# A second seven-product group in the output projection, and a new order of each layer's last stretch

## The chip, the cores and the metric

The program runs on one core of a Trainium2 chip. The metric is the device time of one execution in microseconds, as the median of the runs shown; less is better. TensorE is called PE below, VectorE DVE, ScalarE ACT, GpSimd POOL and SyncE SP, as in the profile.

## The reference, cut to what matters

Two layers of a decoder trunk over 256 tokens and 2048 features, all in float32. Each layer ends with three branch products, a merge with sigmoid gates, and one output projection:

```python
y_a = (dsa_attention(...) * jax.nn.silu(za)) @ w_a_out
y_b = (conformer_conv(...) * jax.nn.silu(zb)) @ w_b_out
y_c = (stick_breaking_attention(...) * jax.nn.silu(zc)) @ w_c_out
g = jax.nn.sigmoid(gates).reshape(b, s, N_BRANCH, D_MODEL)
merged = g[:, :, 0] * y_a + g[:, :, 1] * y_b + g[:, :, 2] * y_c
return x + merged @ w_out                    # (256, 2048) @ (2048, 2048)
```

After the second layer comes a final RMSNorm. The change is in how `merged @ w_out` is computed, and in what stands around it.

## The kernel before, in words

**Precision.** A float32 product is made of three float32r products: each weight block is split on the chip into a high part `wh` (ACT, a cast, line 255 in `high`) and a low part `wl` (DVE, a subtraction, line 259 in `low`), each activation into `hi` and `lo`, and PE adds hi x wh, lo x wh and hi x wl (`mult`, line 270).

**Steps.** The work on weights is a list of steps which `run` goes through in order. A step takes one 512 KB weight block (2 x 128 rows, 512 columns). A plain step (`plain`) is a full one: two halves of the tokens, so 3 x 2 x 2 = 12 matmuls of 128x128x512, the last 4 of which read `wl`. `run` asks for the loads some 7 steps ahead (into 5 `raw` buffers and, each sixth, `va`) and splits the blocks 2 steps ahead. `wh` and `wl` have 3 buffers each, so the split of a step can be written only when PE has read that of the step three before.

**Seven products.** `Seven` computes a 2 x 2 x 2 block product (1024 rows, two halves of the tokens, two chunks of 512 columns) by seven products M1 to M7 in place of eight. Each is cut into two half steps, a and b, of 6 matmuls each, the last 2 of which read `wl`. A half step needs a split of its own, and the group needs sums of weight blocks (`first_sums`, `second_sum`, `last_sum`: by DVE, or by a DMA that accumulates, issued by POOL, depending on `adds` and `room`) and sums of activations (`osums`, from `output_sums`). Its four PSUM banks are X, Y, Z and W: ACT copies X to Y after M1 and W to an SBUF tile after M5, and DVE makes Z after M6 and W after M7 (`fork`, line 581), each from that tile and Y.

**The output projection before.** It has four chunks of 512 columns, q = 0 to 3. One group `o` takes the upper 1024 rows of two chunks (`p0` and `p0 + 1`: 2 and 3 in the first layer, 0 and 1 in the last); their lower rows are plain steps. The other two chunks, `c` and `d`, are 8 plain steps each, in PSUM tiles of two banks (`wide_accs`). In the last layer the lower half of chunk 3 is done after `run`, in a tail that ends with the norm and the stores.

**What comes just ahead.** The products with `w_b_out` (`y1`, 4 chunks of 4 plain steps; the last is called y15 below) and the gates' group `h1` with its plain steps `e1` and `f1`. When a chunk of `y1` is done, `merged` multiplies and adds on DVE (lines 1568, 1569), transposes on DVE (line 299, two rows), goes through DRAM by POOL's DMAs (`z`, then `zy`), and is split by ACT and DVE (`use_m`, line 668) into `mx`, which the output projection reads.

**The order.** The order of the steps is written out by hand in strings for `gather`. From there a scheduler sets the order on each engine; an engine goes through its own instructions strictly in that order. SP and POOL issue the DMAs from queues of the same kind.

Of the kernel before, what the change touches and what calls it, by code (L numbers as in the profile page):

```python
# [30 lines left out]
LATER = 10  # L31
# [20 lines left out]
def trunk(ctx: ExitStack, tc: tile.TileContext, x, w_in, xt, w_a, w_b, w_c, w_out,  # L52
# [73 lines left out]
    def part(b, i, k, n=1, ts=slice(0, S)):  # L126
        return b[k // 4][:, k % 4:k % 4 + n, i, ts]
# [178 lines left out]
    def back(z, y):  # L306

        nc.gpsimd.dma_start(y.rearrange("p (t a) k i -> p t (a k i)", a=4), z.rearrange("t b c a e -> (b c) t (a e)"))  # L308

    def turned(srcs, use, later=LATER, tmp=None, soon=False):  # L310


        n = len(srcs)
        if tmp is None:
            tmp = tp.tile([P, n * 512], F32, tag="zt", bufs=1, name=nm("zt"))
        c = srcs[0].shape[1]
        z = away([v.rearrange("p (k e) -> p k e", e=P) for v in srcs], tmp[:, :n * c], soon)
# [110 lines left out]
    def plain(w, k0, c0, act, banks, start, stop, nk=2):  # L428
        st = Step(lambda: raw_unit(w, k0, c0), None)

        def mm(w_):
            for i, j in ((0, 0), (1, 0), (0, 1)):
                for t, bank in enumerate(banks()):
                    for k in range(2):
                        a = part(act, i, k0 + k, 1, slice(t * P, (t + 1) * P))[:, 0, :]
                        m = mult(bank, a, w_[j][:, k, :], start and i + j + k == 0, stop and j == 1 and k == 1)
            return m

        st.mm = mm
# [19 lines left out]
    class Seven:  # L459


        def __init__(self, w, cols, act, sums, lead=7, own=None, adds=False, room=None):
            self.banks = banks = {}
            self.steps = {}

            def bank(n):
                if n not in banks:
                    banks[n] = acc_tile()
                return banks[n]

            self.bank = bank
# [117 lines left out]
    def gather(spec, **named):  # L589

        lists = {n: list(v) for n, v in named.items() if isinstance(v, list)}
        out = []
        for word in spec.split():
            n, _, many = word.partition("*")
            if n in lists:
                for _ in range(int(many or 1)):
                    out.append(lists[n].pop(0))
            else:
                g, p = n.split(".")
                out += [named[g][p, h] for h in range(2)] if len(p) == 2 else [named[g][p[:2], "ab".index(p[2])]]  # L600
        assert not any(lists.values()), {n: len(v) for n, v in lists.items()}
        return out
# [166 lines left out]
    for layer in range(DEPTH):  # L769
        w = w_in[layer]  # L770
# [4 lines left out]
        sums = parts(KC)  # L775
# [429 lines left out]
        def turn_first():  # L1205
            with in_turn():
# [6 lines left out]
                   g=u, y=keys, c=ug, d=ua))  # L1213
# [162 lines left out]
        room = [once(lambda: slot().rearrange("p a b -> p (a b)")) for _ in range(2)]  # L1376
# [12 lines left out]
        qs = chunk_steps(w, O_QC + 4 * P, hx, KD, lambda a: turned(a, partial(use_q, 4)))  # L1389
# [85 lines left out]
        def sticks(stick=stick, attended=attended):  # L1475
            while len(attended) < 2 * NT:
                yield 1
            for h0 in range(0, NH, 4):
# [5 lines left out]
                   g=kg, q=qs, y=za, c=kc_, d=kd_, z=zb, v=vs))  # L1484
# [86 lines left out]
        for j in range(2):  # L1571
            g = chunk_N(w, [(O_G + j * 512, 512)], hx, KD)
# [6 lines left out]
        last = layer == DEPTH - 1  # L1579
# [44 lines left out]
        wc, wb, wo = w_c[layer], w_b[layer], w_out[layer]  # L1624
# [9 lines left out]
        def merged(b, j, y):  # L1634
            sg = held.pop((b, j), None)
            with in_turn() if b == 1 else nullcontext():
                merge(b, j, y, sg)
            if b == 1:
                with in_turn():
                    turned([mg(j, t) for t in range(NT)], partial(use_m, j), LATER - 3 * (j == 3 and not last), soon=True)  # L1640

        kept_x, acc3 = {}, once(wide_accs)

        def output(q, banks, k0):
            if last and q == 3:
                return [plain(wo, k, q * 512, mx, acc3, k == 0, False) for k in range(0, KC, 2)]

            def finished():
                xc = kept_x.pop(q)
                emit_x(xc, banks(), q, q * 512, list(range(NT)))  # L1650
                store_x(xc, q * 512)

            def ask():
                kept_x[q] = residual(q * 512, 512)

            banks = once(banks or wide_accs)
            steps = [plain(wo, k, q * 512, mx, banks, k == 0, k == KD - 2) for k in range(k0, KD, 2)]
            steps[-1].at(1, finished).at(-4, ask)
            return steps

# [25 lines left out]
        p0 = 0 if last else 2  # L1686
        osums = Lazy(2, lambda: parts(4)[0])
# [9 lines left out]
        h1, e1, f1 = gates(1, 2, 7, None, 2)  # L1697
        y0, y2, y1 = ([products(b, wy, j, gx) for j in range(4)] for b, wy, gx in ((0, w_a[layer], ga), (2, wc, gc), (1, wb, gb)))
# [14 lines left out]
        zg["M4", 1].at(1, partial(gate_summed, 0))  # L1713
        zg["M3", 1].at(1, partial(gate_summed, 1))
        for i in range(2):
            y1[3][i].at(0, partial(output_sums, i * 2, i * 2 + 1))
        if last:
            zd[3].at(0, lambda: nc.sync.dma_start(fwl[0], fnw.partition_broadcast(P)))
        o = Seven(wo, (p0 * 512, p0 * 512 + 512), mx, osums, 10, None, 3)
        qs = {}  # L1720
        for q in range(4):
            own = q in (p0, p0 + 1)
            banks = (lambda v: lambda: [o.bank(n) for n in v])("ZW" if q - p0 else "XY") if own else None
            qs[q] = output(q, banks, KC if own else 0)
# [12 lines left out]
        steps += gather("y g.M1a y g.M5a g.M1b y g.M5b y g.M6a y g.M6b y g.M2a c g.M2b c g.M7a c g.M7b c g.M4a d g.M4b d g.M3a d g.M3b d",  # L1737
                        g=zg, y=y2[4:10], c=zc, d=zd)
        steps += gather(thin + rest, y=y2[10:], g=g1, c=c1, d=d1)
        steps += gather("y*2 " + begin.replace("M6a y", "M6a").replace("M2a y", "M2a") + rest, g=h1, y=y1[:8], c=e1, d=f1)  # L1740
        steps += y1[8:]
        def no_products():
            with in_turn():
                for f in halves:
# [5 lines left out]
        steps[12].at(0, lambda: urgent.__setitem__(0, True), True)  # L1750
        steps[steady - 1].at(0, lambda: urgent.__setitem__(0, False))
        steps[at_norm].at(0, norm)
        c, d = 2 - p0, 3 - p0
        if last:
            steps += qs[c][:4] + gather(
                "g.M1a d g.M5a g.M1b d g.M5b d g.M6a d g.M6b c g.M2a c g.M2b g.M7a g.M7b g.M3a e g.M3b e g.M4a f g.M4b f c*2 e*2 f*2",
                g=o, c=qs[c][4:], d=qs[d], e=qs[p0], f=qs[p0 + 1])
        else:
            steps += qs[c][:4] + qs[d][:4] + gather(
                "g.M1a c g.M5a g.M1b c g.M5b d g.M6a d g.M6b c g.M2a c g.M2b d g.M7a d g.M7b g.M3a g.M3b e g.M4a e g.M4b e*2 f*4",  # L1760
                g=o, c=qs[c][4:], d=qs[d][4:], e=qs[p0], f=qs[p0 + 1])
# [13 lines left out]
        with tc.high_priority(offset=URGENT):  # L1775
            nc.vector.reduce_sum(known, ssq[:, :, :3], axis=AX.X)
            nc.vector.tensor_scalar(half, known, -0.5 / D, -0.5 * EPS, op0=ALU.mult, op1=ALU.add)
            nc.vector.tensor_scalar(known, known, 1.0 / D, EPS, op0=ALU.mult, op1=ALU.add)

        c0, n = 1536, 512  # L1780
        xc = residual(c0, n)

        head = acc3()
        accs = [head[0], acc_tile()]
        nc.vector.tensor_add(xc[:, 1, :], head[1], xc[:, 1, :])
        oh, ol = ([slot(F32R).rearrange("p (k a) t -> p k (a t)", a=2) for _ in range(2)] for _ in range(2))
# [3 lines left out]
        for t in range(NT):  # L1790
            m, r, b = (small(1) for _ in range(3))
# [93 lines left out]
```

## Time and profile before

| | |
|---|---|
| median of 3 runs | 1980.36 us (1979.25 to 1982.67) |
| the profiled execution | 1980.07 us, its span 1978.3 us |
| PE busy in the span | 1965.0 us (99%) |
| DVE busy | 1714.5 us (87%) |
| granted PE clock over the span | 0.998 |

The time of the profiled execution is 1.8 us longer than its span, and it is 0.3 us below the median. PE's records are modelled at their ends, so how long a matmul takes is read from the distance between the starts of two groups, and where PE stood still from its waits.

### The profile page before, as it was taken

What the parts mean: (1) busy time and instruction counts of PE and PEld (TensorE: products, weight loads), DVE (VectorE), ACT (ScalarE), POOL (GpSimd) and SP (SyncE); (2) the same over time, 40 slices, a digit from 0 to 9 for tenths busy, and PEclk for the clock granted to TensorE, in tenths of its full rate; (3) what the DMA queues carried; (4) which work ended last, traced back from release to release, by engine and by line L of the source; (5) the groups of instructions that cost most, each with busy time, mean ns of one, the idle gap of its engine ahead of it and who ended that gap; (6) DMA issues with size and microseconds to landing.
All of it is one profiled execution on the core that took longest, in us unless ns stands there. A gap on an engine that the chain in (4) does not pass through costs nothing.

```text
span 1978.3 us, 26294 instructions
## 1 busy us (share of the span) xinstructions
PE 1965.0 (99%) x9170; PEld 1645.4 (83%) x9170; DVE 1714.5 (87%) x2010; ACT 1356.9 (69%) x1778; POOL 249.3 (13%) x348
## 2 busy tenths in 40 slices
PE   9999999999999999999999999999999999999998
PEld 8888887888888888888888888888888888888886
DVE  8798998988999989878786988999889988898786
ACT  7567657679888666565565666576798886665654
POOL 0021112210200002111200211122101000011010
PEclk9999999999999999999999999999999999999999
DMA  7888759876889899887978887598659798899883
GB/s 277 279 259 265 238 180 305 269 233 189 249 241 271 245 262 286 271 269 270 320 234 272 246 276 234 181 309 277 223 175 285 241 297 239 253 293 271 275 290 135
DMA packets 256261, 503.67 MB, mean 255 GB/s; under 512 B 18496, under 2 KB 31296, under 8 KB 256000
## 3 DMA queue, kind: packets, MB, share of 16 engines
q1 hardware_dynamic: 218560, 408.13, 62.2%
q0 software_dynamic: 35904, 90.72, 18.3%
q10 hardware_dynamic: 1664, 3.15, 0.4%
q8 instruction: 71, 1.16, 0.2%
q14 instruction: 62, 0.51, 0.1%
HBM read 469.16 MB, written 32.77 MB: 254 GB/s over the span
## 4 chain that ended last, share of the span: by engine, by line
PE 97%; DMA 1%; DVE 1%; ACT 0%; issue 0%; DVEq 0%; ACTq 0%
PE acc L270 66%; PE mm L270 28%; DMA raw<-in_w_in_dram 1%; PE mm L1269 1%; PE mm L1360 0%; DVE wl L259 0%; PE mm L1411 0%; PE mm L1464 0%; DMA va<-in_w_in_dram 0%; PE mm L1441 0%; PE mm L1327 0%; PE mm L918 0%; PE mm L1240 0%; PE mm L1330 0%; PE mm L1414 0%; PE mm L1469 0%
## 5 line engine op out<-in xcount | busy, mean ns | idle before, releaser
L270 PE MATMUL acc<-wh,s 128*128 128x512 f32 x3952 | 1006.1, 390 | 0.6 <-ACT wh L255 0.6
L255 ACT CAST wh<-raw 128x1024 fp32r<-128x1024 f32 (+1 forms) x637 | 665.1, 1047 | 394.0 <-PE acc L270 251.6
L259 DVE TENSOR_TENSOR wl<-raw,wh 128x1024 fp32r<-128x1024 f32 (+1 forms) x638 | 770.5, 1214 | 165.0 <-ACT wh L255 162.8
L270 PEld LDWEIGHTS acc<-wh,s 128*128 128x128 f32 x3952 | 735.2, 188 | 149.4 <-ACT wh L255 1.4
L270 PE MATMUL acc<-wl,s 128*128 128x512 f32 x1784 | 499.5, 390 | 2.3 <-DVE wl L259 2.3
L270 PEld LDWEIGHTS acc<-wl,s 128*128 128x128 f32 x1784 | 333.6, 188 | 74.1 <-DVE wl L259 5.4
L270 PE MATMUL mm<-wh,s 128*128 128x512 f32 (+1 forms) x1504 | 366.8, 385 | 0.4 <-ACT wh L255 0.4
L270 PEld LDWEIGHTS mm<-wh,s 128*128 128x128 f32 x1504 | 281.2, 188 | 55.8 <-ACT wh L255 0.9
L302 POOL DMA_DIRECT2D z<-zt x192 | 115.9, 657 | 670.8 <-DVE zt L299 626.0
L270 PE MATMUL mm<-wl,s 128*128 128x512 f32 (+1 forms) x752 | 198.0, 385 | 0.0
L270 PEld LDWEIGHTS mm<-wl,s 128*128 128x128 f32 x752 | 140.8, 188 | 26.9
L255 ACT CAST wh<-ar 128x1024 fp32r<-128x1024 f32 x92 | 97.0, 1054 | 68.3 <-PE acc L270 35.0
L259 DVE TENSOR_TENSOR wl<-ar,wh 128x1024 fp32r<-128x1024 f32 x92 | 112.1, 1222 | 23.7 <-ACT wh L255 20.6
L259 DVE TENSOR_TENSOR wl<-va,wh 128x1024 fp32r<-128x1024 f32 x53 | 64.8, 1222 | 21.8 <-ACT wh L255 21.5
L255 ACT CAST wh<-va 128x1024 fp32r<-128x1024 f32 x53 | 55.6, 1049 | 35.6 <-PE acc L270 17.2
L308 POOL DMA_DIRECT2D zy<-z x50 | 37.1, 743 | 322.2 <-DVE s L668 94.4
L270 PEld LDWEIGHTS mm<-s,wl 128*128 128x128 f32 x512 | 66.9, 191 | 5.0
L733 DVE SCALAR_TENSOR_TENSOR s<-yT,cst,s 128x256 f32<-128x256 f32 x160 | 69.8, 483 | 0.0
L270 PE MATMUL mm<-s,wl 128*128 128x192 f32 x512 | 66.0, 271 | 0.0
L728 ACT ACTIVATE ar<-yT,cst 128x256 f32<-128x256 f32 x136 | 60.5, 503 | 2.9 <-PE mm L1330 2.3
L728 ACT ACTIVATE zt<-yT,cst 128x256 f32<-128x256 f32 x128 | 57.6, 503 | 4.9 <-DVE s L1037 4.9
L530 POOL DMA_DIRECT2D ar<-in_w_in_dram x28 | 33.7, 1212 | 190.9 <-DVE wl L259 190.9
(293 smaller groups left out, 1587.0 us busy)
## 6 DMA issues: line engine op xcount, KB each, us to landing
raw<-in_w_in_dram SPq DMA_DIRECT2D x496, 512.0 KB, 4.6
raw<-in_w_out_dram SPq DMA_DIRECT2D x50, 512.0 KB, 5.4
zy<-z POOLq DMA_DIRECT2D x48, 512.0 KB, 5.9
z<-zt POOLq DMA_DIRECT2D x184, 128.0 KB, 5.3
ar<-in_w_in_dram SPq DMA_DIRECT2D x28, 512.0 KB, 6.9
ar<-in_w_in_dram POOLq DMA_DIRECT2D x28, 512.0 KB, 8.6
raw<-in_w_a_dram SPq DMA_DIRECT2D x26, 512.0 KB, 6.7
raw<-in_w_b_dram SPq DMA_DIRECT2D x26, 512.0 KB, 4.9
```

What stands on the lines that cost most here:

```text
L255: newest_parts[0] = nc.scalar.copy(u[1], u[0])
L259: newest_parts[1] = sub = nc.vector.tensor_sub(u[2], u[0], u[1].bitcast(F32))
L270: newest[0] = nc.tensor.matmul(o, lhsT, rhs, start=start, stop=stop, skip_group_check=True)
L302: nc.gpsimd.dma_start(z[:, :, :, a, :].rearrange("t b c e -> c (t b) e"), tmp[a * 32:(a + 1) * 32].rearrange("c t b k i -> c (t b) (k i)"))
L308: nc.gpsimd.dma_start(y.rearrange("p (t a) k i -> p t (a k i)", a=4), z.rearrange("t b c a e -> (b c) t (a e)"))
L530: nc.gpsimd.dma_start((homes if own is None else third)[h], block(1, 0, h), accum_op=ALU.add)
L728: nc.scalar.activation(v, yT[:, c, q:q + S], AF.Identity if bias else AF.Copy, scale=wq, **b)
L733: nc.vector.scalar_tensor_tensor(o, yT[:, c, q:q + S], wq, o, op0=ALU.mult, op1=ALU.add)
L1269: nc.tensor.matmul(ps[:, q * S:(q + 1) * S], qi[i][:, hd, :], ki[j][:, 0, :], start=n == 0, stop=n == 2)
```

## The change

A second group, `n`, does the upper 1024 rows of chunks `c` and `d`, so that all four chunks have their upper rows by seven products. `n` uses the buffers that `o` used (`ar`, `ph`, `pl`) and four single PSUM banks; `o` moves to two slots of the activations' pool (`places`, called s8 below), its first sum is partly done by an accumulating DMA (`adds` 2 in place of 3), and its banks are the halves of two wide tiles. `n` begins before `y1` is done: the last four steps of `y1` stand between its half steps. The merge of chunk 1 is asked to come back earlier, and `output_sums` moves to the steps `f1[2]` and `f1[3]`. The last layer's tail reads its bank from `n`.

```diff
-        def __init__(self, w, cols, act, sums, lead=7, own=None, adds=False, room=None):
+        def __init__(self, w, cols, act, sums, lead=7, own=None, adds=False, room=None, wide=False):
...
                 if n not in banks:
-                    banks[n] = acc_tile()
+                    if wide:
+                        banks.update(zip("XY" if n in "XY" else "ZW", wide_accs()))
+                    else:
+                        banks[n] = acc_tile()
                 return banks[n]
...
-                    turned([mg(j, t) for t in range(NT)], partial(use_m, j), LATER - 3 * (j == 3 and not last), soon=True)
+                    turned([mg(j, t) for t in range(NT)], partial(use_m, j), LATER - 3 * (j in (1, 3)), soon=True)
...
-        def output(q, banks, k0):
+        def output(q, banks):
             if last and q == 3:
-                return [plain(wo, k, q * 512, mx, acc3, k == 0, False) for k in range(0, KC, 2)]
+                return []
...
-            steps = [plain(wo, k, q * 512, mx, banks, k == 0, k == KD - 2) for k in range(k0, KD, 2)]
+            steps = [plain(wo, k, q * 512, mx, banks, False, k == KD - 2) for k in range(KC, KD, 2)]
...
-            y1[3][i].at(0, partial(output_sums, i * 2, i * 2 + 1))
+            f1[2 + i].at(0, partial(output_sums, i * 2, i * 2 + 1))
...
-        o = Seven(wo, (p0 * 512, p0 * 512 + 512), mx, osums, 10, None, 3)
+        c, d = 2 - p0, 3 - p0
+        places = [once(lambda: slot().rearrange("p a b -> p (a b)")) for _ in range(2)]
+        o = Seven(wo, (p0 * 512, p0 * 512 + 512), mx, osums, 10, None, 2, places, True)
+        n = Seven(wo, (c * 512, d * 512), mx, osums, 10, None, 3)
...
-        steps += gather("y*2 " + begin.replace("M6a y", "M6a").replace("M2a y", "M2a") + rest, g=h1, y=y1[:8], c=e1, d=f1)
-        steps += y1[8:]
+        steps += gather("y*2 " + begin.replace("M6a y", "M6a").replace("M2a y", "M2a") +
+                        "g.M3a c g.M3b c g.M4a c g.M4b c y*4 d*4", g=h1, y=y1[:12], c=e1, d=f1)
...
+        second = "n.M1a y n.M5a y n.M1b y n.M5b y n.M6a n.M6b n.M2a n.M2b n.M7a n.M7b "
         if last:
-            steps += qs[c][:4] + gather(
-                "g.M1a d g.M5a g.M1b d g.M5b d g.M6a d g.M6b c g.M2a c g.M2b g.M7a g.M7b g.M3a e g.M3b e g.M4a f g.M4b f c*2 e*2 f*2",
+            second += ("o.M1a c o.M5a c o.M1b o.M5b n.M3a n.M3b o.M6a o.M6b n.M4a n.M4b o.M2a c o.M2b c "
+                       "o.M7a o.M7b o.M3a e o.M3b e o.M4a f o.M4b f e*2 f*2")
         else:
-            steps += qs[c][:4] + qs[d][:4] + gather(
-                "g.M1a c g.M5a g.M1b c g.M5b d g.M6a d g.M6b c g.M2a c g.M2b d g.M7a d g.M7b g.M3a g.M3b e g.M4a e g.M4b e*2 f*4",
+            second += ("o.M1a c o.M5a d o.M1b c o.M5b d o.M6a n.M4a o.M6b n.M4b c*2 o.M2a d o.M2b n.M3a n.M3b d "
+                       "o.M7a o.M7b o.M3a e o.M3b e o.M4a e o.M4b e f*4")
+        steps += gather(second, n=n, o=o, y=y1[12:], c=qs[c], d=qs[d], e=qs[p0], f=qs[p0 + 1])
...
-        head = acc3()
+        head = [n.bank(i) for i in "ZW"]
```

The built programs have 9097 matmuls before and 9073 now. Lines of `Seven` and of what stands between it and `output` are 3 higher in the changed kernel: the fork is line 584, the splits of `use_m` line 671, the merge lines 1571 and 1572, the sums lines 514 and 529.

What moves on two engines is shown at one place of the first layer, from y15 on; the second layer has the same DVE rows there.

On DVE the changed program has these rows just behind the split of y15. They are the splits of n.M2a (raw_1466), n.M2b (raw_1470), n.M7a (ph) and n.M7b (pl), the merge of y15's chunk (L1571, L1572), the fork of Z (L584) and the two transposes.

```order
L259 TENSOR_TENSOR wl_1485_8061<-raw_1466_7972,wh_1484_8060 128x1024
L1571 TENSOR_TENSOR t4_1459_7938<-mm_1462_7946,t4_1459_7938 128x1024
L259 TENSOR_TENSOR wl_1489_8081<-raw_1470_7992,wh_1488_8080 128x1024
L1572 TENSOR_TENSOR s8_956_5412<-s8_956_5412,t4_1459_7938 128x1024
L584 TENSOR_TENSOR acc_1490_8090<-ev_1479_8036,acc_1474_8006 128x512
L299 STREAM_TRANSPOSE zt_1486_8072<-s8_956_5412 128x4x4x32 x2
L259 TENSOR_TENSOR wl_1494_8100<-ph_1415_7693,wh_1493_8099 128x1024
L259 TENSOR_TENSOR wl_1497_8113<-pl_1430_7766,wh_1496_8112 128x1024
```

In the program before, a merge fell among full steps; here it stands between the splits of six half steps that follow each other without a full step.

The next rows on DVE of the changed program: sums for `o` (L514, L529), the fork of W (L584), the splits of o.M1a (raw_1480), of a full step of `c` (raw_1483), of o.M5a (s8_1471), of a full step of `d` (raw_1492) and of o.M1b (va_1495), and the low part of an earlier chunk's `mx` (L671).

```order
L514 TENSOR_TENSOR s8_1471_7994<-s8_1471_7994,raw_1480_8038 128x1024
L584 TENSOR_TENSOR acc_1465_7965<-ev_1479_8036,acc_1474_8006 128x512
L259 TENSOR_TENSOR wl_1500_8126<-raw_1480_8038,wh_1499_8125 128x1024
L259 TENSOR_TENSOR wl_1503_8138<-raw_1483_8057,wh_1502_8137 128x1024
L259 TENSOR_TENSOR wl_1506_8151<-s8_1471_7994,wh_1505_8150 128x1024
L259 TENSOR_TENSOR wl_1509_8163<-raw_1492_8095,wh_1508_8162 128x1024
L529 TENSOR_TENSOR s8_1471_7994<-s8_1467_7974,raw_1480_8038 128x1024
L514 TENSOR_TENSOR s8_1471_7994<-s8_1471_7994,va_1495_8109 128x1024
L259 TENSOR_TENSOR wl_1511_8180<-va_1495_8109,wh_1510_8179 128x1024
L671 TENSOR_TENSOR s8_1491_8092<-zy_1452_7899,s8_1491_8092 128x4x256
```

All of them are new at this place: before, `o` stood alone, among plain steps.

For comparison, DVE in the program before, around the old group's M6a (the first ar), M6b (the second ar), M2a (raw_1512) and M2b (raw_1520).

```order
L526 TENSOR_TENSOR ar_81<-pl_1471_8002,raw_1485_8084 128x1024
L259 TENSOR_TENSOR wl_1517_8241<-ar_81,wh_1516_8240 128x1024
L668 TENSOR_TENSOR s8_1519_8252<-zy_1495_8142,s8_1519_8252 128x4x256
L259 TENSOR_TENSOR wl_1522_8258<-va_1502_8173,wh_1521_8257 128x1024
L259 TENSOR_TENSOR wl_1525_8276<-ar_81,wh_1524_8275 128x1024
L259 TENSOR_TENSOR wl_1527_8286<-raw_1508_8205,wh_1526_8285 128x1024
L259 TENSOR_TENSOR wl_1531_8306<-raw_1512_8219,wh_1530_8305 128x1024
L581 TENSOR_TENSOR acc_1532_8315<-ev_1518_8250,acc_1511_8217 128x512
L259 TENSOR_TENSOR wl_1534_8318<-raw_1515_8238,wh_1533_8317 128x1024
L259 TENSOR_TENSOR wl_1537_8337<-raw_1520_8255,wh_1536_8336 128x1024
L259 TENSOR_TENSOR wl_1540_8349<-raw_1523_8273,wh_1539_8348 128x1024
```

Every second split there is that of a full step (va_1502, raw_1508, raw_1515, raw_1523).

On PE the changed program has this order from n.M7a's last matmuls to the end of o.M1b (mm_1507 and mm_1512 are banks of `o`, wh_1496 is n.M7b, wh_1502 the step of `c`, wh_1505 o.M5a, wh_1508 the step of `d`, wh_1510 o.M1b); ahead of them stand the 24 matmuls of n.M6 and n.M2, then 4 of n.M7a and 4 of o.M1a with `wh`.

```order
L270 MATMUL acc_1474_8006<-wl_1494_8100,s8_1450_7893 128x512 x2
L270 MATMUL acc_1474_8006<-wh_1496_8112,s8_1450_7893 128x512 x4
L270 MATMUL acc_1474_8006<-wl_1497_8113,s8_1450_7893 128x512 x2
L270 MATMUL acc_1458_7931<-wh_1502_8137,s8_1491_8092 128x512 x2
L270 MATMUL acc_1474_8006<-wh_1502_8137,s8_1491_8092 128x512 x2
L270 MATMUL mm_1512_8183<-wh_1505_8150,s8_1451_7896 128x512 x4
L270 MATMUL mm_1507_8154<-wl_1500_8126,s8_1408_7672 128x512 x2
L270 MATMUL acc_1490_8090<-wh_1508_8162,s8_1491_8092 128x512 x2
L270 MATMUL acc_1465_7965<-wh_1508_8162,s8_1491_8092 128x512 x2
L270 MATMUL mm_1512_8183<-wl_1506_8151,s8_1451_7896 128x512 x2
L270 MATMUL mm_1507_8154<-wh_1510_8179,s8_1408_7672 128x512 x4
L270 MATMUL mm_1507_8154<-wl_1511_8180,s8_1408_7672 128x512 x2
```

Steps are taken apart here: the remaining 8 matmuls of the step of `c` and the 8 of the step of `d` stand behind o.M1b. In the second layer the 2 `wl` matmuls of o.M5a come right behind those of o.M1a, no step of `d` is among them, and behind o.M1b comes one matmul of o.M5b and then the 8 of `c`.

Before, PE had whole steps one after the other around the old group's M2a (wh_1530) and M2b (wh_1536).

```order
L270 MATMUL mm_1474_8008<-wh_1526_8285,s8_1519_8252 128x512 x8
L270 MATMUL mm_1474_8008<-wl_1527_8286,s8_1519_8252 128x512 x4
L270 MATMUL acc_1501_8166<-wh_1530_8305,s8_1441_7836 128x512 x4
L270 MATMUL acc_1501_8166<-wl_1531_8306,s8_1441_7836 128x512 x2
L270 MATMUL mm_1474_8008<-wh_1533_8317,s8_1519_8252 128x512 x8
L270 MATMUL mm_1474_8008<-wl_1534_8318,s8_1519_8252 128x512 x4
```

A half step and a full step take turns.

## Rows read from the trace of the kernel before

**Rows 1.** The page: busy time of two engines, and the chain that ended last.

```profile
PE 1965.0 (99%) x9170; PEld 1645.4 (83%) x9170; DVE 1714.5 (87%) x2010; ACT 1356.9 (69%) x1778; POOL 249.3 (13%) x348
...
PE 97%; DMA 1%; DVE 1%; ACT 0%; issue 0%; DVEq 0%; ACTq 0%
```

**Rows 2.** Waits of PE, whole span: us in total, times, longest.

```profile
PE acc L270 <- DVE wl L259: 2.3, 3, 1.6
PE mm L918 <- DVE eps L79: 1.1, 1, 1.1
PE acc L270 <- ACT wh L255: 0.6, 1, 0.6
PE mm L270 <- ACT wh L255: 0.4, 1, 0.4
PE mm L1441 <- DVE pl L668: 0.2, 1, 0.2
```

**Rows 3.** Windows over both last stretches: busy us per engine, clock, DMA, GB/s.

```profile
883.50:989.60 106.10, 106.10 (x470) 87.74 (x469) 87.57 (x90) 60.58 (x72) 17.03 (x26) 1.00 0.88 294
1863.40:1958.40 95.00, 95.00 (x421) 78.57 (x420) 79.66 (x82) 55.28 (x64) 8.56 (x12) 1.00 0.76 249
```

**Rows 4.** PE and ACT in order of time: a full step, then a half step.

```profile
950.02 1.98 PE L270 MATMUL mm<-wh,s 128*128 128x512 f32 x8
...
951.84 1.07 PE L270 MATMUL mm<-wl,s 128*128 128x512 f32 x4
952.04 1.05 ACT L255 CAST wh<-ph 128x1024 fp32r<-128x1024 f32 x1 [1.21 <-PE mm L270]
952.74 1.07 PE L270 MATMUL acc<-wh,s 128*128 128x512 f32 x4
...
953.65 0.62 PE L270 MATMUL acc<-wl,s 128*128 128x512 f32 x2
...
954.10 1.98 PE L270 MATMUL mm<-wh,s 128*128 128x512 f32 x8
```

**Rows 5.** DVE in order of time, around a merge of `y1`.

```profile
905.49 1.23 DVE L259 TENSOR_TENSOR wl<-raw,wh 128x1024 fp32r<-128x1024 f32 x1 [1.50 <-ACT wh L255]
906.63 1.22 DVE L1568 TENSOR_TENSOR t<-mm,t 128x1024 f32<-128x1024 f32 x1
907.88 1.22 DVE L1569 TENSOR_TENSOR s<-s,t 128x1024 f32<-128x1024 f32 x1
909.02 1.22 DVE L259 TENSOR_TENSOR wl<-raw,wh 128x1024 fp32r<-128x1024 f32 x1
910.16 1.30 DVE L299 STREAM_TRANSPOSE zt<-s 128x512 f32<-128x512 f32 x2
911.38 1.18 DVE L259 TENSOR_TENSOR wl<-raw,wh 128x1024 fp32r<-128x1024 f32 x1
```

**Rows 6.** What DVE waited for from 880 to 1010 us: total, times, longest.

```profile
DVE wl L259 <- ACT wh L255: 18.4, 17, 1.5
```

**Rows 7.** What SP's queue waited for, 880 to 1010 us.

```profile
SPq L425 <- DVE wl L259: 66.0, 29, 5.3
```

**Rows 8.** DMA, 880 to 1010 us: GB/s in 40 slices; median us to landing.

```profile
GB/s 171 176 345 345 239 233 306 284 330 384 398 390 339 117 174 155 156 229 248 203 214 323 388 324 273 222 186 352 405 405 386 389 404 372 220 258 361 147 132 263
...
raw<-in_w_out_dram SPq DMA_DIRECT2D x25, 512.0 KB, 5.5
...
zy<-z POOLq DMA_DIRECT2D x6, 512.0 KB, 6.9
...
ar<-in_w_out_dram POOLq DMA_DIRECT2D x2, 512.0 KB, 9.5
```

More of the change, by code (lines that the diff above doesn't have):

```diff
@@ L1639, in merged @@
                 with in_turn():
-                    turned([mg(j, t) for t in range(NT)], partial(use_m, j), LATER - 3 * (j == 3 and not last), soon=True)
-        kept_x, acc3 = {}, once(wide_accs)
-        def output(q, banks, k0):
+                    turned([mg(j, t) for t in range(NT)], partial(use_m, j), LATER - 3 * (j in (1, 3)), soon=True)
+        kept_x = {}
+        def output(q, banks):
             if last and q == 3:
-                return [plain(wo, k, q * 512, mx, acc3, k == 0, False) for k in range(0, KC, 2)]
+                return []
             def finished():
@@ L1654, in ask @@
                 kept_x[q] = residual(q * 512, 512)
-            banks = once(banks or wide_accs)
-            steps = [plain(wo, k, q * 512, mx, banks, k == 0, k == KD - 2) for k in range(k0, KD, 2)]
+            steps = [plain(wo, k, q * 512, mx, banks, False, k == KD - 2) for k in range(KC, KD, 2)]
             steps[-1].at(1, finished).at(-4, ask)
@@ L1715, in trunk @@
         for i in range(2):
-            y1[3][i].at(0, partial(output_sums, i * 2, i * 2 + 1))
+            f1[2 + i].at(0, partial(output_sums, i * 2, i * 2 + 1))
         if last:
             zd[3].at(0, lambda: nc.sync.dma_start(fwl[0], fnw.partition_broadcast(P)))
-        o = Seven(wo, (p0 * 512, p0 * 512 + 512), mx, osums, 10, None, 3)
[L1720 to L1724, printed above, removed]
+        c, d = 2 - p0, 3 - p0
+        places = [once(lambda: slot().rearrange("p a b -> p (a b)")) for _ in range(2)]
+        o = Seven(wo, (p0 * 512, p0 * 512 + 512), mx, osums, 10, None, 2, places, True)
+        n = Seven(wo, (c * 512, d * 512), mx, osums, 10, None, 3)
+        qs = {q: output(q, lambda g=g, v=v: [g.bank(i) for i in v])
+              for q, g, v in ((c, n, "XY"), (d, n, "ZW"), (p0, o, "XY"), (p0 + 1, o, "ZW"))}
         begin = "g.M1a y g.M5a g.M1b y g.M5b y g.M6a y g.M6b y g.M2a y g.M2b y g.M7a y g.M7b "
@@ L1752, in trunk @@
         steps[at_norm].at(0, norm)
-        c, d = 2 - p0, 3 - p0
+        second = "n.M1a y n.M5a y n.M1b y n.M5b y n.M6a n.M6b n.M2a n.M2b n.M7a n.M7b "
         if last:
-            steps += qs[c][:4] + gather(
-                "g.M1a d g.M5a g.M1b d g.M5b d g.M6a d g.M6b c g.M2a c g.M2b g.M7a g.M7b g.M3a e g.M3b e g.M4a f g.M4b f c*2 e*2 f*2",
-                g=o, c=qs[c][4:], d=qs[d], e=qs[p0], f=qs[p0 + 1])
-        else:
-            steps += qs[c][:4] + qs[d][:4] + gather(
-                "g.M1a c g.M5a g.M1b c g.M5b d g.M6a d g.M6b c g.M2a c g.M2b d g.M7a d g.M7b g.M3a g.M3b e g.M4a e g.M4b e*2 f*4",
-                g=o, c=qs[c][4:], d=qs[d][4:], e=qs[p0], f=qs[p0 + 1])
+            second += ("o.M1a c o.M5a c o.M1b o.M5b n.M3a n.M3b o.M6a o.M6b n.M4a n.M4b o.M2a c o.M2b c "
+                       "o.M7a o.M7b o.M3a e o.M3b e o.M4a f o.M4b f e*2 f*2")
+        else:
+            second += ("o.M1a c o.M5a d o.M1b c o.M5b d o.M6a n.M4a o.M6b n.M4b c*2 o.M2a d o.M2b n.M3a n.M3b d "
+                       "o.M7a o.M7b o.M3a e o.M3b e o.M4a e o.M4b e f*4")
+        steps += gather(second, n=n, o=o, y=y1[12:], c=qs[c], d=qs[d], e=qs[p0], f=qs[p0 + 1])
         extra = []
```

## The prediction

> **What bounds the kernel now.** I read the page first. PE is busy 99% of the span and stands for 97% of the chain that ended last [rows 1]: whatever takes matmuls away shortens the time, as long as everything else keeps up. Next come PE's waits. The whole span has only three waits for a `wl`, 2.3 us together, and the other rows are smaller [rows 2]: the kernel hides nearly all splits, sums and transfers, and any wait that is new comes fully on top. The windows over the stretches that change show how near the next engine is: DVE is busy 87.57 of 106.1 us in the first layer and 79.66 of 95.0 in the last, at a granted clock of 1.00 in both [rows 3]. ACT, third in these rows, has much more room (60.58 and 55.28). Then the prices. On PE 8 matmuls take 951.84 - 950.02 = 1.82 us and the 4 `wl` ones 0.90, so a full step 2.72 and a matmul 0.2267; a half step (952.74 to 954.10) is 1.36 [rows 4]. On DVE a row of 1024 elements lasts 1.22 us, but the next row that does not need its result starts 1.13 to 1.14 later, and two transposes of 512 take 1.22, so 0.61 each [rows 5]. A split therefore costs DVE 1.135 us, which is 42% of a full step's time on PE and 83% of a half step's.
>
> **Removed: 24 matmuls.** 9097 - 9073 = 24, 12 in each layer, at 0.2267: 5.44 us. PE bounds both stretches, so this is worth its full price if nothing comes late. The group `n` has 14 half steps (84 matmuls) where 8 plain steps (96) were.
>
> **Added: DVE rows.** A half step needs a split as large as that of a full step, so 8 splits become 14, and the group brings its forks and sums. Over both layers DVE has 27 rows more. At 1.135 that is at most 30.6 us, on top of 87.57 + 79.66 = 167.2: 197.9 us of work against 201.1 - 5.4 = 195.7 us of PE time. On average DVE would have no slack left in these stretches. It can take some from its waits for `wh`, 18.4 us in the 130 us around the first one [rows 6], if it can run ahead; but three `wh` and three `wl` buffers let a split lead by two or three steps, and a lead of three half steps is only 4 us. So the average is not the question; the densest place is.
>
> **The densest place.** It lies behind y15. Set zero where PE leaves y15. Seven half steps follow without a full one (n.M6a, M6b, M2a, M2b, M7a, M7b, o.M1a). The order shows what DVE must do meanwhile, strictly in turn: from the split of n.M2a to L671, 19 rows. Fifteen have 1024 elements (9 splits, the 2 merge rows, 3 sums, L671); four have 512 (2 forks, 2 transposes). That is 15 x 1.135 + 4 x 0.61 = 19.47, and 0.09 more because the last is wanted at its end (1.22): 19.56 us.
>
> It can't start much before zero. The third split behind y15's, n.M2a's, goes into y15's own `wh` and `wl`. PE reads that `wh` until its last 4 matmuls, 0.9 before zero; the cast then takes 1.05 [rows 4] and DVE starts at 0.2 plus a signal, 0.4. If ACT is one copy behind, 1.0. I take 0.7 between the two. The run then ends at 20.26 and the split of o.M1b, the row ahead of L671, at 19.1.
>
> PE wants them earlier. In the first layer the order gives 12 + 12 + 4 + 4 matmuls, then the 28 rows shown down to o.M1b's `wh`: 60 x 0.2267 = 13.60 for the split of o.M1b, and 62 x 0.2267 = 14.06 for L671, which the other 8 matmuls of `c` read (lo x `wh`). PE is late by 20.26 - 14.06 = 6.2 us (5.9 to 6.5 for the two starts). In the second layer no step of `d` stands between, and one matmul of o.M5b stands ahead of the 8 of `c`: 59 x 0.2267 = 13.38, late by 6.9 (6.6 to 7.2). The lateness comes in pieces (the split of n.M7a, row 8, ends at 8.3 and is wanted at 32 x 0.2267 = 7.25), but the pieces add up to that of the last row, since PE, once held, is held less by the next. Sum: 6.2 + 6.9 = 13.1 us (12.5 to 13.7). Nothing gives it back, as PE has no other idle time.
>
> PE can't work around it. Its queue is in order, so what stands behind o.M1b's `wl` matmuls waits with them. In the Trainium skill "TensorE: Matmul & The Clock Gate", section "Part 3: Packing small matmuls — row/col tiling", says that matmuls run in program order and only weight loads are pulled ahead. By that rule the ready matmuls of `c` and `d` give no relief; if they could pass, some 16 of them (3.6 us) would go ahead in the first layer. No row of the kernel before shows either.
>
> **Edits that I cost at nothing.** Moving `output_sums` to `f1` and the interleaving of `y1`'s last four steps: ACT and DVE do this among steps that are two or three ahead; if that lead is gone, the run above starts later, at a full price of one row (1.1 us) for each row too many. The wide banks for `o`: the same bytes of PSUM, free by then. More DMA: some 6 transfers of 512 KB a layer, 3.1 MB on top of 106.1 us x 294 GB/s = 31.2 MB, so 34.3 MB in some 103 us, 332 GB/s; slices of 405 GB/s occur before [rows 3, 8], so it fits. Without cover it would be 3.1 MB at 405, 7.8 us a layer at most. SP's queue waits for raw buffers alone, that is for DVE [rows 7], so a late DVE delays loads too, but these are asked for some seven steps ahead against 5.5 us to landing [rows 8]. The accumulating transfers take 9.5 and the way back of `zy` 6.9 [rows 8]. There is one `zy`, and the last chunk's way back waits for L671 of the one before, which stands at the end of the late run: at my count it lands with about 1 us to spare. At nothing in the sum, 0 to 2 us a layer in the range. The tail is the same work from another bank: 0.
>
> **Sum.** 1980.07 (the profiled execution, 0.3 below the median of the runs) - 5.44 + 13.1 = 1987.7; against the median, 1987.8 with half of the 0.3 kept. I give 1987.8.
>
> **Rivals.**
> *The saving shows in full (the other side).* Before, DVE did merges, sums and splits without holding PE: the merge at 906.63 stands in an unbroken row of work [rows 5] and the three waits of the whole span are 2.3 us [rows 2]. If DVE's lead at y15 covers the run, it comes to 1980.07 - 5.44 = 1974.6. Against it: the lead can't be longer than the buffers, as the split of n.M2a needs y15's. It decides at 2.72 us of lateness a layer (5.44 / 2): below that the kernel is faster. The run would have to be 3 to 4 rows shorter (6.2 - 2.72 = 3.5, at 1.135) for even, 6 for the full saving.
> *The lateness is half as large.* If the sums (3 rows) come before the splits in time, or PE itself arrives later for another reason that the matmuls removed do not touch, 6.6 in all remain: 1980.07 - 5.44 + 6.6 = 1981.2, no change.
> *It gets worse than the sum.* Two ways. First, DVE's rows follow each other at their full duration: the row at 907.88 needs the result of 906.63 and starts 1.25 after it, not 1.14 [rows 5]. The new run has sums whose results the next row reads. With 1.22 for all 15 and 0.65 for the four it is 20.9 in place of 19.56, 1.3 more a layer, 1990.4. Second, `zy` comes late, up to 2 us a layer, 1991.8. Both: 1994. In the Trainium skill "VectorE: DVE Perf Modes", section "The DRAIN you can't avoid", states that an operation does not begin before the one ahead has drained. By that rule all rows would be spaced at their durations, with the 1990.4 just given; the independent rows, 1.14 apart at 1.22 each, do not agree, the dependent pair does.
>
> **How the numbers follow.** My forecast (DVE's run late in both layers, 1984.5 to 1990.5: a row or two less a layer at the low end, `zy` at the high end) has 0.65; the full or nearly full saving 0.09; half the lateness 0.09; worse than the sum 0.17. Some 0.2%, 4 us, is what a measurement here tells from no change. So faster 0.09, same 0.10, slower 0.81. The range leaves out the full saving and the last of the worst case: 1981 to 1993.
>
> **What the profile of the changed kernel would show.** Right: 24 matmuls fewer; PE's waits of some 6 to 7 us in each layer in the first 20 us behind y15, at `wl` (L259) of n.M7a, o.M1a, M5a or M1b and at L671, none longer than 3; there DVE without a gap, its waits for `wh` gone, 19 rows in 19 to 20 us; elsewhere PE as before; DMA slices at 400 GB/s or less without PE waiting for `raw`. Wrong in size: DVE rows spaced 1.2 or more in that run, or a wait for `zy` ahead of L671. Wrong altogether: PE passes from n.M6a to c's last 8 matmuls in about 14 us, and the span is 5 us shorter; or DVE's 19 rows are spread, because some were done before y15. A wait for `raw` or for an accumulating DMA would mean that the transfers, which I cost at nothing, bind.

## The result, and the profile after

The changed kernel takes 1999.5 us (median of 4, 1996.33 to 2000.39) against 1981.02 us (4 runs beside it): ratio 1.0093 (1.0081 to 1.0106), so it is slower, by more than twice what was forecast (1987.8, range 1981 to 1993). The profiled execution took 1999.09 us, 19.0 more than the one of before.

The page and PE's waits of the whole span, answering to [rows 1] and [rows 2]:

```profile
PE 1972.8 (99%) x9146; PEld 1643.8 (82%) x9146; DVE 1740.3 (87%) x2037; ACT 1369.7 (69%) x1794; POOL 259.2 (13%) x356
```

```profile
PE mm L270 <- DVE wl L259: 3.7, 3, 2.2
PE mm L270 <- DVE mm L584: 3.1, 2, 1.8
PE mm L270 <- ACT wh L255: 1.9, 2, 1.5
PE acc L270 <- ACT wh L255: 1.9, 1, 1.9
PE acc L270 <- DVE wl L259: 1.8, 5, 0.5
PE acc L270 <- DVE acc L584: 1.7, 4, 0.8
```

PE has 24 records fewer and is busy 7.8 us longer: more matmuls it can't be. Some were slower, and as their ends are modelled, the last one before each short wait counts for longer. The windows of the first layer behind y15 (engines in the order PE, PEld, DVE, ACT, POOL, then clock, DMA share, GB/s; [rows 3] is the same view) say where:

```profile
910.00:920.00 10.00, 9.20 (x41) 7.30 (x40) 9.72 (x11) 7.44 (x8) 3.69 (x4) 1.00 1.07 342
920.00:930.00 10.00, 8.41 (x31) 4.92 (x29) 10.00 (x10) 4.20 (x4) 2.36 (x4) 1.00 1.10 264
930.00:940.00 10.00, 8.46 (x24) 6.34 (x25) 7.17 (x7) 3.72 (x4) 0.72 (x1) 0.66 1.02 343
```

Three things stand there. DVE is busy for the whole of 920 to 930 while PE does 31 matmuls where 44 fit. The granted clock is 0.66 from 930 to 940: part of it at the lower level, 1.2 GHz. And the DMA engines are full (1.07 and 1.10) at rates well below 405 GB/s. DVE's rows at the start and the end of its run, in the first layer and in the second:

```profile
913.10 1.23 DVE L259 TENSOR_TENSOR wl<-raw,wh 128x1024 fp32r<-128x1024 f32 x1 [0.21 <-ACT wh L255]
914.24 1.22 DVE L1571 TENSOR_TENSOR t<-mm,t 128x1024 f32<-128x1024 f32 x1
...
930.26 1.22 DVE L259 TENSOR_TENSOR wl<-va,wh 128x1024 fp32r<-128x1024 f32 x1
931.40 1.22 DVE L671 TENSOR_TENSOR s<-zy,s 128x1024 fp32r<-128x1024 f32 x1
...
1901.20 1.23 DVE L259 TENSOR_TENSOR wl<-raw,wh 128x1024 fp32r<-128x1024 f32 x1 [0.21 <-ACT wh L255]
...
1919.49 1.22 DVE L671 TENSOR_TENSOR s<-zy,s 128x1024 fp32r<-128x1024 f32 x1
```

PE, from y15's end (n.M6a starts at 912.07) to the 8 matmuls of `c` that need L671 (932.67) and beyond, with the wait of o.M3a at 971.98; and the first two places in the second layer (1900.74 and 1921.36):

```profile
912.07 1.07 PE L270 MATMUL acc<-wh,s 128*128 128x512 f32 x4
...
928.12 1.19 PE L270 MATMUL mm<-wh,s 128*128 128x512 f32 x4 [0.39 <-ACT wh L255]
931.53 1.22 PE L270 MATMUL mm<-wl,s 128*128 128x512 f32 x2 [2.23 <-DVE wl L259]
932.67 2.07 PE L270 MATMUL acc<-wh,s 128*128 128x512 f32 x4
...
937.84 1.08 PE L270 MATMUL acc<-wl,s 128*128 128x512 f32 x4
...
971.98 1.15 PE L270 MATMUL mm<-wh,s 128*128 128x512 f32 x4 [1.77 <-DVE mm L584]
...
1900.74 1.07 PE L270 MATMUL acc<-wh,s 128*128 128x512 f32 x4
...
1917.32 2.08 PE L270 MATMUL mm<-wh,s 128*128 128x512 f32 x4 [1.50 <-ACT wh L255]
...
1921.36 1.91 PE L270 MATMUL acc<-wh,s 128*128 128x512 f32 x4
1923.06 1.58 PE L270 MATMUL acc<-wl,s 128*128 128x512 f32 x4
1924.48 0.85 PE L270 MATMUL acc<-wh,s 128*128 128x512 f32 x3
```

DVE's run lasts from 913.10 to 932.62, 19.52 us for 19 rows. PE gets to `c` at 932.67 - 912.07 = 20.60 us, 6.5 late, and at 1921.36 - 1900.74 = 20.62 in the second layer, 7.2 late. There the run starts earlier, 0.46 us behind n.M6a's start, and ends at 1920.71 after 19.51 us; the last 0.65 us before `c` are matmuls of `o` at a granted clock of 0.50 (1917.3 to 1921.3). From `c` on PE still crawls in both layers: 12 matmuls take 937.84 - 932.67 = 5.17 us in place of 2.72, and in the second layer 8 take 3.12 in place of 1.81. The DMA queues from 900 to 960 us (packets, MB, share of the 16 engines), and what issues took to land, answering to [rows 8]:

```profile
q1 hardware_dynamic: 6190, 11.93, 59.1%
q0 software_dynamic: 2113, 4.72, 36.0%
...
raw<-in_w_out_dram SPq DMA_DIRECT2D x15, 512.0 KB, 9.2
...
ar<-in_w_out_dram POOLq DMA_DIRECT2D x2, 512.0 KB, 14.3
z<-zt POOLq DMA_DIRECT2D x4, 128.0 KB, 14.1
```

Loads land in 9.2 (before: 6.6 in the same window, 5.5 in that of [rows 8]), and `z`, the first half of a chunk's way through DRAM, in 14.1 (before: 5.4). POOL's queue (q0, six of its transfers accumulating) used 0.360 x 60 / 4.72 = 4.6 us of all engines for a MB, SP's (q1, plain loads) 3.0.

### The profile page after: what moved, and what is told of

Same layout as the page of the kernel before. It is cut to its first block, busy times and chain, and to the rows that moved or that the text cites. A ratio compares the mean times of both kernels' runs of the same rounds, so it can differ in the third digit from the quotient of the medians.

```text
span 1997.0 us, 26327 instructions
## 1 busy us (share of the span) xinstructions
PE 1972.8 (99%) x9146; PEld 1643.8 (82%) x9146; DVE 1740.3 (87%) x2037; ACT 1369.7 (69%) x1794; POOL 259.2 (13%) x356
## 4 chain that ended last, share of the span: by engine, by line
PE 49%; DVE 1%; ACT 0%; issue 0%; DVEq 0%; ACTq 0%
PE acc L270 32%; PE mm L270 15%; DVE wl L259 0%; PE mm L1272 0%; PE mm L1363 0%; ACT wh L255 0%; PE mm L1467 0%; PE mm L1414 0%; PE mm L1330 0%; DVE s L514 0%; PE mm L1444 0%; DVE s L1831 0%; PE mm L1243 0%; PE mm L1333 0%; PE mm L1472 0%
## 5 line engine op out<-in xcount | busy, mean ns | idle before, releaser
L255 ACT CAST wh<-raw 128x1024 fp32r<-128x1024 f32 x635 | 662.0, 1046 | 367.5 <-PE acc L270 236.9
L270 PE MATMUL mm<-wh,s 128*128 128x512 f32 (+1 forms) x1520 | 374.9, 387 | 5.0 <-DVE mm L584 3.1
L270 PE MATMUL mm<-wl,s 128*128 128x512 f32 (+1 forms) x760 | 203.9, 387 | 3.7 <-DVE wl L259 3.7
```

The lines of the kernel that those rows point to most:

```text
L255: newest_parts[0] = nc.scalar.copy(u[1], u[0])
L270: newest[0] = nc.tensor.matmul(o, lhsT, rhs, start=start, stop=stop, skip_group_check=True)
```

## The experiments

**First theory:** DVE's run of 19 rows holds PE, the low clock follows from the waits, and o.M3a waits for a fork because Z and W share a tile now. **Rivals:** the transfers bind; DVE's total binds, whatever the order; the clock falls by itself. "Before" was 1980.3 to 1981.9 in all comparisons.

**e1_later.** One number: L671 of chunk 2 goes ahead of the run.

```diff
-  partial(use_m, j), LATER - 3 * (j in (1, 3)), soon=True)
+  partial(use_m, j), LATER - 3 * (j > 0), soon=True)
```

> One number is changed: the way back of chunk 2 of the merged product is asked for 3 steps earlier, so that its low part (L671) stands on DVE ahead of the split of y15 and not as the last of the 19 rows behind it. No row is taken away. Theory (the last row of DVE's run holds PE, and the ready matmuls of c and d stand behind it): PE can do 16 matmuls (3.6 us) of c and d ahead of o.M1b, which is then late by about 1 us in each layer in place of 6.5 and 7.2; without the long waits the clock stays at 1.00, which gives back 3.9 us. 1999.5 - 5.5 - 6.2 - 3.9 = about 1984 (1982 to 1988). Rival (DVE's total is what binds: 27 rows more in stretches where it has no slack): the rows are all there still, so less than 3 us is won, 1996 to 2000. Rival (transfers bind): no change.

2002.1 us (1999.9 to 2003.1): nothing won. The mechanism came out as expected, and something else took its place. PE has no wait above 0.2 us from 918 to 937, the matmuls of `c` and `d` run ahead of o.M1b; then it stands for 6.2 us. PE's longest wait there, what ACT and POOL do at that time, and two windows:

```profile
PE mm L270 <- ACT wh L255: 6.2, 1, 6.2
```

```profile
935.09 0.72 POOL L308 DMA_DIRECT2D zy<-z  x1 [13.60 <-DMA z<-zt]
...
941.75 1.04 ACT L670 CAST s<-zy 128x1024 fp32r<-128x1024 f32 x1 [7.66 <-DMA zy<-z]
942.70 1.04 ACT L255 CAST wh<-s 128x1024 fp32r<-128x1024 f32 x1
```

```profile
920.00:930.00 10.00, 10.00 (x44) 7.96 (x45) 10.00 (x10) 5.52 (x6) 1.49 (x3) 1.00 1.11 253
930.00:940.00 10.00, 7.60 (x34) 5.97 (x32) 5.25 (x5) 2.18 (x3) 0.72 (x1) 1.00 1.01 364
940.00:950.00 10.00, 6.20 (x21) 5.07 (x22) 6.22 (x6) 7.27 (x8) 2.41 (x2) 0.66 0.38 82
```

POOL waits 13.6 us for `z` to land before it can issue `zy`; ACT stands at the cast of chunk 3 for 7.7, and the casts for PE queue behind it. In the changed kernel the same cast comes at 941.25, behind a wait of 2.16, and holds nobody, because PE is late by then (it has no gap from 940 to 950). In the second layer e1 has a wait of 4.3 us for a split, queued on DVE behind a residual (L1785) whose load took 17 us to land.

**e2_skip5.** Five DVE rows fewer in each run.

```diff
+  for g, p in ((n, "M2"), (n, "M7"), (o, "M1")):
+      for h in range(1 if g is o else 2):
+          g[p, h].bare = True        # third product reads wh, no split by DVE
```

> The low splits of five half steps in the dense place (n.M2a, M2b, M7a, M7b, o.M1a) are left out; their third product reads the high part, so the output is not the reference's; matmuls, transfers and orders stay. Theory (DVE's run is the cause): 5 x 1.135 = 5.7 us less run in each layer, lateness 0.9 and 1.5 left, the low clock gone: 1999.5 - 11.4 - 3.9 = about 1984 (1982 to 1988). Rival (the transfers, 1.05 to 1.10 of the DMA engines' time behind y15, or the wide banks): the bytes and the banks are the same, so the time stays at 1996 or more.

1998.1 us (1996.1 to 2001.3). The first theory alone falls again, as the rival of the transfers had it; in the first layer PE waits once, 7.2 us, for a cast that stands behind chunk 3's, which waits 10.8 for `zy`.

**e3_cover.**

```diff
-  o.M2b n.M3a n.M3b d o.M7a o.M7b o.M3a e
+  o.M2b n.M3a n.M3b o.M7a o.M7b d o.M3a e
```

(and the last `c` likewise in the second layer)

> The last full step of d (first layer) and of c (second layer) stands between o.M7b and o.M3a, where after has o.M7b and o.M3a one behind the other; nothing else moves. Theory (o.M3a waits for the fork of W since Z and W are now halves of one wide tile, and PE has nothing in between): the two waits of 1.8 and 1.3 us for L584, with 0.3 us of slower first matmuls, go: 1999.5 - 3.4 = 1996.1 (1995 to 1997.5). Rival (DVE is behind at that place anyway): the wait moves to the next split, no change, 1998.5 to 2000.5.

1993.7 us (1988.9 to 1996.4), 5.8 less. PE has no wait for L584 on a wide tile any more. The forecast was 3.4; the rest lies within the spread of its four runs (7.6 us). The trace is of its fastest run (1988.9), where the granted clock over the span is 0.998, against 0.995 in after's.

**e4_filler.**

```diff
   for i, j in ((0, 0), (1, 0), (0, 1)):
+      for _ in range(j * fill.get((name, h), 0)):
+          mult(bank("Y"), ..., w_[0][:, 0, :], True, True)
...
+  o.fill.update({("M5", 0): 12, ("M1", 1): 2} if last else {("M1", 1): 10})
```

> 24 matmuls that compute nothing (they write the bank Y of o before it is made) stand in PE's waits: 10 ahead of the wl matmuls of o.M1b in the first layer, 12 ahead of those of o.M5a and 2 ahead of those of o.M1b in the second. 24 x 0.2267 = 5.4 us of work. Theory (PE waits there for DVE, and the low clock follows from the waits): the work costs nothing, the granted clock stays at 1.00, and the 2.5 and 1.4 us that the low clock costs come back: 1999.5 - 3.9 = 1995.6 (1994.5 to 1997). Rival (the clock falls at that place for another reason): no change, 1999.5. Rival (PE itself is the bound there): 5.4 us more, 2005.

1996.1 us (1995.3 to 1997.0): 24 matmuls more, 3.4 us less. PE and a window of the first layer:

```profile
926.25 3.47 PE L270 MATMUL mm<-wh,s 128*128 128x512 f32 x14 [0.39 <-ACT wh L255]
929.67 0.73 PE L270 MATMUL mm<-wl,s 128*128 128x512 f32 x2
930.81 1.19 PE L270 MATMUL acc<-wh,s 128*128 128x512 f32 x4 [0.40 <-DVE s L675]
931.84 1.08 PE L270 MATMUL acc<-wl,s 128*128 128x512 f32 x4
```

```profile
930.00:940.00 10.00, 9.60 (x42) 7.62 (x41) 6.01 (x6) 4.92 (x6) 0.72 (x1) 1.00 0.95 333
```

The ten matmuls fill the wait, `c` starts just as late (20.58 us behind n.M6a's start, 20.60 in after), and the clock stays at 1.00, where after has 0.66. So the waits bring the low clock, and the low clock is worth what its rows say.

**Second theory:** two limits stand side by side, DVE's run and a late `z`; each hides the other. **Rival:** the transfers alone.

**e5_noacc, e6_later_noacc.** Four accumulating transfers a layer out, of the changed kernel and of e1_later.

```diff
   def first_adds(h):
+      if "first" in bare: return     # set for o
...
   def last_sum(h):
+      if "last" in bare: return      # set for n
```

> Of the changed kernel, four of its accumulating transfers of 512 KB in each layer are left out (the last sum of n into ar, the first sum of o into its slot); the output is not the reference's; DVE, ACT and PE have the same rows in the same order. Theory now (two limits stand side by side: DVE's run of 19 rows, and DMA engines that are full behind y15, where the way back of chunk 3 lands 14 us late): with the transfers relieved the run of DVE still holds PE by 6.5 and 7.2 us, so 1995 to 2000. Rival (the transfers alone are the cause, and DVE's run only looks late): all waits go, 1985 or less. Rival (transfers don't matter): 1999.5.

> The same four transfers a layer left out (the output is not the reference's), and the way back of chunk 2 asked for 3 steps earlier as in e1_later. Theory (two limits side by side, each hides the other): with both relieved, only the waits for the forks (3.4 us) and some 3 us of small ones stay: 1980.3 - 5.4 + 6.4 = about 1981 (1978 to 1986), where each alone gives 1995 to 2002. Rival (a third thing makes ACT wait for the way back of chunk 3): still 1995 or more.

1996.2 us (1993.2 to 1999.0) and 1986.1 us (1982.7 to 1988.6, 10 runs). With after and e1 this is a square: neither, 1999.5; L671 earlier alone, 2002.1; transfers relieved alone, 1996.2; both, 1986.1. One alone makes it 2.6 us slower, the other alone 3.3 faster, both 13.4 faster: both limits are shown. The 1986.1 is 5 us above the forecast for e6, just outside its range. PE's waits from 905 to 1010 us in e6:

```profile
PE mm L270 <- DVE mm L589: 1.8, 1, 1.8
PE acc L270 <- DVE acc L589: 0.4, 1, 0.4
```

**e8_plain.** Which property of those transfers costs?

```diff
-  nc.gpsimd.dma_start(third[h], block(0, 1, h), accum_op=ALU.add)
+  nc.gpsimd.dma_start(third[h], block(0, 1, h), **({} if "first" in bare else dict(accum_op=ALU.add)))
```

(and `last_sum` of n likewise)

> As e1_later, but the four accumulating transfers a layer that e6_later_noacc leaves out are plain ones here: the same queue, bytes, places and waits, with nothing added on the way (the output is not the reference's). If the kind costs (an accumulating transfer holds the DMA engines longer for the same bytes: in e1_later from 900 to 960 us POOL's queue took 36.5% of the engines for 4.72 MB, SP's 54.3% for 11.42 MB), the time comes near that without them: 1986 to 1992. If only the bytes cost, or the place behind them in the queue: 1998 to 2003, as e1_later.

1985.6 us (1984.8 to 1988.1, 10 runs): the same bytes from the same queue cost nothing once they don't add. From 900 to 960 us, and the window to hold beside those of after and e1:

```profile
q1 hardware_dynamic: 6801, 13.11, 64.9%
q0 software_dynamic: 1751, 5.16, 28.6%
...
z<-zt POOLq DMA_DIRECT2D x8, 128.0 KB, 5.9
```

```profile
920.00:930.00 10.00, 10.00 (x44) 8.00 (x44) 10.00 (x10) 5.54 (x6) 2.22 (x4) 1.00 0.85 286
```

POOL's queue uses 0.286 x 60 / 5.16 = 3.3 us of the engines for a MB (4.6 in after and in e1), `z` lands in 5.9 (chunk 3's four writes in 5.3), and from 920 to 930 more bytes move with the engines less full.

**e9_zqueue.**

```diff
-  nc.gpsimd.dma_start(z[...], ...)
+  (nc.sync if soon else nc.gpsimd).dma_start(z[...], ...)
```

> As e1_later, but the first half of the merged chunks' way through DRAM (z from zt) is issued from SP's queue in place of POOL's. If z lands 14 us late because it stands behind three accumulating transfers in POOL's queue, it lands in some 6 us, the wait of 6.2 us in the first layer and the low clock behind it go: 1989 to 1994. If all DMA engines are full, whatever the queue: within 3 us of e1_later (1999 to 2005).

1990.0 us (1989.2 to 1996.3), 12 less than e1, inside the forecast. The trace is of its slowest run, 1996.3, where PE still waits 2.7 and 5.8 us for casts that stand behind chunk 3's. In it `z` lands in 10.3 us, not 6: the queue is part of it, the full engines another. The Trainium skill, "DMA: Bandwidth & Descriptors", section "Issuing engines are not separate DMA queues", holds that all issuing engines share the 16 DMA engines and that issuing from several saves only issuing time. That the engines are shared agrees with `z` still taking 10.3. On what a change of queue saves, the measured 12 us are more than issuing time, and the measurement decides. How much of the 12 comes from `z`'s own queue is not shown: with `z` gone from it, POOL also issues the sums into `ar` earlier, 6.3 us ahead of the transposes in place of 1.8.

**e7_both, e10_both2, e11_both3, e12_both3z.** Attempts at a better kernel: e1, e3, o's loads asked for earlier, the residual row in the last layer behind the splits.

```diff
-  o = Seven(wo, ..., mx, osums, 10, None, 2, places, True)
+  o = Seven(wo, ..., mx, osums, 22, None, 2, places, True)   # e10: 16 if last; e11, e12: 16
-  LATER - 3 * (j in (1, 3))
+  LATER - 3 * (j > 0)            # e10: + 2 * (last and j == 2); e11, e12: + 2 * (j == 2)
+  with issue_after(newest_parts[1].ins):
       nc.vector.tensor_add(xc[:, 1, :], head[1], xc[:, 1, :])
```

> Nothing left out. On top of e1_later: the full step between o.M7b and o.M3a as in e3_cover; the loads and accumulating transfers of o asked for 22 steps ahead in place of 10, so that they lie before the full stretch of the DMA engines; in the last layer the row that adds the residual to a bank of n stands behind the last split on DVE. Theory (two limits, and both relieved): 1980.3 - 5.4 + some 3 us of small waits = about 1978 (1975 to 1984). Rival (earlier loads only move the full stretch of the DMA engines): 1990 or more.

> As e7_both, with two numbers of the last layer mended, where e7_both waited 3.5 us for the way back of chunk 2: there o's loads are asked for 16 steps ahead (22 in the first layer), and the split of that chunk stands 2 steps later on ACT. Theory (the two limits, with no third): that wait and the low clock behind it (3.4 us) go, 1989.5 - 6.9 = about 1982.5 (1979 to 1986), which is no gain over the kernel before, since some 6 us of small waits for DVE use up the 5.4 saved. Rival (the full stretch of the DMA engines only moves on): 1987 or more.

> As e10_both2, with the last layer's two numbers (o's loads 16 steps ahead, the split of chunk 2 two steps later) in the first layer too, where e10_both2 waited 2.8 us for that chunk and the clock was at 0.5 for 3.4 us behind it. Theory: that goes, 4.5 us less, 1986.3 - 4.5 = about 1982 (1979 to 1985), even with the kernel before or a little behind it. Rival (the full stretch of the DMA engines, held by accumulating transfers, gives another late transfer): 1986 or more.

> As e11_both3, with z issued from SP's queue as in e9_zqueue, where that was worth 12 us against e1_later. Theory: in e11_both3 the transfers are early enough, so it is worth nothing, and DVE's order is a little worse: 1983 to 1987. Rival (z behind accumulating transfers still holds PE): faster than e11_both3 by 2 us or more.

1989.5, 1986.3, 1985.0 and 1987.0 us. e7 and e10 missed their ranges, in the way of the rival: with the loads earlier, the full stretch of the DMA engines lies earlier (a share of 1.05 to 1.09 from 890 to 905 us in e10, 0.55 to 0.90 in e1) and makes another way back late. ACT's wait in e10's first layer:

```profile
ACT s L670 <- DMA zy<-z: 5.5, 1, 5.5
```

e11 takes most of what can be had: 14.5 us less than after, with a ratio of 1.0022 (1.0010 to 1.0033) to the kernel before, still behind it. In e12 `z`'s queue is worth nothing once the loads lie earlier: 2 us slower than e11, with chunk 3's `z` landing in 8.1 from SP's queue and in 4.9 from POOL's. No version here beats the kernel before.

## Why the prediction was wrong

- **DVE's run: right, to 0.7 us.** 6.2 and 6.9 us of lateness were forecast, 6.5 and 7.2 measured; the run started at 1.03 (first layer) and 0.46 (second) where 0.7 was taken, and took 19.52 and 19.51 in place of 19.56. In the second layer it accounts for 6.6 of the 7.2; the rest is the low clock, two points further on. Rows followed each other 1.13 to 1.14 apart at a duration of 1.22, so the rival of full durations fell. The prediction took half of what the Trainium skill says for it: "VectorE: DVE Perf Modes", section "The DRAIN you can't avoid", also has that an operation which is not held starts earlier, and the spacing here agrees with that.
- **"PE can't work around it": right.** The ready matmuls waited behind o.M1b; in e1, where the order lets them go ahead, that wait went.
- **No term for the clock: the first step that failed.** The sum counted the waits and not what PE does after them. From the rows, 5.17 - 2.72 + 3.12 - 1.81 = 3.8 us from `c` on; e4, which keeps the clock up, gave back 3.4.
- **"The wide banks for o: the same bytes of PSUM, free by then": the second.** The bytes were free, but Z and W are halves of one tile now, and o.M3a, which writes Z, waits for the fork that writes W: 1.77 and 1.34 us. Before, with four single banks, M3a stood right behind M7b too and no such wait was there [rows 2]. e3 put a step between and removed the waits; whether the chip or the program's own ordering by tiles makes the wait was not tried. This step and the clock are 6.9 of the 11.4 us between the forecast for the profiled execution (1987.7) and 1999.1.
- **"332 GB/s; slices of 405 GB/s occur before, so it fits": the third, and it alone costs as much (e1).** The engines were full at 264 GB/s. Accumulating transfers hold them longer, which the rate of plain ones does not show (e8). The trace of before had it: where POOL's queue carries the old group's two accumulating transfers and nothing else, the engines are full at 230 GB/s, and a MB takes 0.584 x 10 / 1.01 = 5.8 us of all engines against 0.426 x 10 / 1.29 = 3.3 for SP's loads beside it. In the changed kernel this lies behind DVE's lateness; it is what keeps a remedy for DVE from paying (e1, e2), and it is a second limit, not a term to add. Before, from 940 to 950 us:

```profile
940.00:950.00 10.00, 10.00 (x45) 8.27 (x45) 7.37 (x7) 5.35 (x6) 1.59 (x2) 1.00 1.01 230
```

```profile
q0 software_dynamic: 514, 1.01, 58.4%
q1 hardware_dynamic: 667, 1.29, 42.6%
```

- **The sum with what was measured:** 1980.07 - 5.44 + 6.5 + 7.2 + 3.8 + 3.1 = 1995.2, against 1999.1 profiled. The same matmuls in both traces say where the other 3.9 us lie. The first of line 1499 (1502 in the changed kernel) starts at 686.64 and 686.88 us, that of line 803 (806) at 1004.88 and 1014.67, and the first of line 1499 in the second layer at 1666.47 and 1676.87. So 0.2 us arose ahead of the change and 0.6 between the two stretches; the first stretch cost 9.55 net, 1.5 more than its terms. Some 3 us thus lie in and behind the stretches in pieces that were not followed one by one (0.7 of waits for splits ahead of y15, a slower first matmul after each wait), and their cause stays open.
- **The rivals:** the full saving did not come, and DVE's total is not the bound by itself: e6 has all its rows and is 13.4 us faster. That a late `zy` costs up to 2 us a layer was too small: PE waits 6.2 (e1) and 7.2 us (e2) when DVE lets it show.

What stays open: of the 8.5 us by which e11 misses the full saving (1985.0 against 1981.9 - 5.4), its profile names 4.5 us of PE's waits in the two stretches; e6 misses it by 11.0 (1986.1 against 1980.6 - 5.4), and its profile names 5.7. So the two limits are not all that separates the change from its saving.

## What to carry to other kernels

Before adding work that makes PE's steps shorter, write down the rows of the next engine in queue order between two points, and do the same for the DMA queues with the engine time of each kind of transfer, not with bytes. When one limit is relieved and nothing happens, look for a second that had been hidden, and test the two together: here each alone gave -3 to +3 us and both gave -13. A row that others queue behind (a cast or a split that waits for a transfer) belongs as late in its queue as its own reader allows; this follows from e1's wait and was not tried by itself.

## What was not expected of the hardware

- An accumulating transfer of 512 KB is dearer than a plain one of the same bytes from the same queue: making four of six plain changed a queue from 4.6 to 3.3 us of all DMA engines per MB, and the time of e1_later from 2002.1 to 1985.6 us.
- The granted clock fell to its lower level though no single wait of PE in that stretch was longer than 2.23 us, and matmuls that compute nothing, put into the waits, kept it up.
- Moving the small writes of `z` (four to a merged chunk, 16 a layer) to another queue was worth 12 us in e9 and nothing in e12, where `o`'s transfers are asked for earlier. What makes the difference was not isolated.
